# Seven-product block matmuls in fp32r pairs: the last four products of 31 output pairs take the high and low part of h side by side in one 512-column matmul

## The chip, the cores and the metric

One core of a Trainium2 chip runs the program. The metric is the device time of one execution in microseconds; three timed runs of the kernel before are given. Inputs lie in device memory as fp32, transposed and cut into tiles on the host beforehand.

## The reference, cut to what matters

```python
h = rmsnorm(x, norm_g[l])                       # x: 512 tokens x 2048
(a_q, a_ckv, i_q, i_k, i_w, a_gate, b_q, b_k, b_v, b_gate,
 c_q, c_gate, mix_gate) = split_cols(h @ w_in[l], IN_SIZES)
...
oa = dsa_attention(qa, ka, va, iq, ik, iw, bias_a, topk) * jax.nn.silu(a_gate)
ob = sliding_window_attention(qb, kb, vb, sinks_b[l], bias_b) * jax.nn.silu(b_gate)
oc = memory_attention(qc, kc, vc) * jax.nn.silu(c_gate)
g_a, g_b, g_c = jnp.split(jax.nn.sigmoid(mix_gate + gate_bias[l]), N_BRANCH, axis=-1)
merged = g_a * (oa @ w_up_a[l]) + g_b * (ob @ w_up_b[l]) + g_c * (oc @ w_up_c[l])
x = x + merged @ w_o[l]
```

Most of the arithmetic is `h @ w_in`: 2048 by 11856 weights on 512 tokens. The change is in that product.

## The kernel before

**Precision.** Every fp32 operand of a large product is split into a high part, rounded to fp32r, and a low part, the rest. A product of two such operands is three matmuls: high x high, high x low, low x high (`mm3`, lines 293 to 296: L294 is wh with the high part of h, L295 wh with its low part, L296 wl with the high part). Weights are split as they stream in (`split`): ACT rounds a 128x512 piece to `wh` (L276) and DVE subtracts to get `wl` (L278), four pieces ahead of TensorE (`LA = 4`), six buffers each.

**Seven products.** Outputs come in pairs of two 128-row tiles (transposed: rows are output columns of w_in, columns are tokens). `pair` splits the pair and the 2048-long contraction into 2x2 blocks and forms them from seven block products instead of eight (`PRODS`): each product is 8 k-tiles of 128, three matmuls of 256 columns each, so 168 matmuls a pair. The weight sums that the scheme needs (S1 to S4, tiles `wS`, `wA`, `wraw`) are made on the way in, by POOL (L212) and by accumulating DMAs that POOL issues (L218). Four products read `hth`/`htl` (h itself and one difference), three read the `hx` tiles, six 256-column slots for each of 8 k-tiles: slots 0 to 2 high, 3 to 5 low parts of the sums T2, T3, T4.

The products take the three PSUM banks a, b, c in turn, in the first 256 columns of each. Products 0 to 2 open a bank; 3 to 5 add on top of 0 to 2; 6 opens one again. After each product `evac` (lines 792 to 810) takes what it needs: product 0 is copied to u1 and product 2 to u5 (ACT), product 1 gives u2 (DVE, L796); product 3 is copied to the first half of the first output (ACT, L801); product 4 gives u3 (DVE, L804), and POOL the second half of the second output (L805); product 5 plus u2 is the second half of the first output and product 6 plus u3 the first half of the second (both DVE, L790, in `add`). Then `fin` goes on: for a gate pair two tanh (ACT, L1232) and two DMAs; for a pair of branch A or B tanh and product (L915, L916), the casts of q (L837 to L840 for B), and the head's attention.

**Order of the work.** `STREAM` is the list of pairs: 1 + 4 pairs for keys and index queries, 4 for branch C, 6 for A and 6 for B, and 24 gate pairs (`mix`) in between and behind. Attention (`a_unit`, `b_unit`, `c_unit`), the top-k selection and smaller chores are generators, advanced one step after each half product by `pump`; a table of delays (`LG`) says how many steps a generator waits between its operations. An evacuation is put off by one half product (`pend`, `flush`): the instructions of product n's evacuation stand after the first half of product n+1 in the order of every engine. Each engine runs its instructions in program order, so a wait on ACT or DVE holds up what stands behind it.

In B's stage the attention of a head stands partly in its own pair and mostly in the gate pair that follows: scores on PE, then L1122 to L1126 on DVE (scale and bias, maximum, sink), exponentials on ACT (L1128), normalising on DVE (L1131 to L1134), transposes on PE (L960), the copy to PT on ACT (L963), and PE's PT,vb matmuls (L299). In A's stage L1023 to L1031 do the same, with the score row normalised at L1031.

Of the kernel before, what the change touches and what calls it, by code (L numbers as in the profile page):

```python
# [12 lines left out]
F32R = mybir.dt.float32r  # L13
# [98 lines left out]
def hybrid_layer(ctx: ExitStack, tc: tile.TileContext, xT, memT, memR, w_g1, w_un, w_up, params, consts, rel1, onehot, out):  # L112
# [24 lines left out]
    def psum(tag, name="p"):  # L137
        return ps.tile([128, 512], F32, tag=tag, name=nm(name), bufs=2 if tag == "qk" else 1)
# [20 lines left out]
    gk = cst.tile([128, 3], F32, name="gk")  # L159
    nsink = cst.tile([128, HB], F32, name="nsink")  # L160

    hth = hp.tile([128, KT, T], F32R, name="hth")
    htl = hp.tile([128, KT, T], F32R, name="htl")
    hxt, hxf = {}, {}

    def hx_new(k, dt):
# [126 lines left out]
    def mm3(o, ah, al, bh, bl, first, last, n1=None):  # L293
        pe.matmul(o, ah, bh, start=first, stop=False, skip_group_check=True)  # L294
        pe.matmul(o, ah, bl, start=False, stop=False, skip_group_check=True)  # L295
        pe.matmul(o, al, bh, start=False, stop=last, skip_group_check=True)  # L296
# [39 lines left out]
    def tl(tag, shape=(128, 512), dt=F32):  # L336
        return ws["pool"].tile(list(shape), dt, tag=tag, name=nm(tag), bufs=ws["bufs"][tag])
# [393 lines left out]
    def hpart(name, k):  # L731
# [6 lines left out]
        i = int(name[1]) - 2  # L738
        return hxt[k][:, i, :], hxt[k][:, 3 + i, :]

    prod = [0]
    pend = []

# [33 lines left out]
            onto(x1[:, lo], p, dve)  # L777
            put(1, lo)

    def pair(z0, z1, fin, onto=None):  # L780

        ev = {}
        o = {}

        def e(name):
            ev[name] = stp("ev").tile([128, 256], F32, tag="ev", bufs=4, name=nm(name))
            return ev[name]

        def add(t, p, u):
            dve.tensor_tensor(out=t, in0=p, in1=ev[u], op=ALU.add)  # L790

        def evac(n, p):
            if n == 0:
                act.copy(e("u1"), p)
            elif n == 1:
                dve.tensor_tensor(out=e("u2"), in0=ev["u1"], in1=p, op=ALU.subtract)  # L796
            elif n == 2:
                act.copy(e("u5"), p)
            elif n == 3:
                o[0] = z0()  # L800
                act.copy(o[0][:, :256], p)  # L801
            elif n == 4:
                o[1] = z1()
                dve.tensor_tensor(out=e("u3"), in0=p, in1=ev["u1"], op=ALU.subtract)  # L804
                pool_e.tensor_tensor(out=o[1][:, 256:], in0=ev["u3"], in1=ev["u5"], op=ALU.subtract)  # L805
            elif n == 5:
                add(o[0][:, 256:], p, "u2")
            else:
                add(o[1][:, :256], p, "u3")
                fin(o[0], o[1])  # L810

        bank = {}
        for n, (_, hn, first) in enumerate(PRODS):
            b = "abc"[prod[0] % 3]
            prod[0] += 1
            if first:
                bank[b] = psum(b)[:, :256]
            p = bank[b]
            for half in range(2):
                wh, wl = next_hb()  # L820
                for kk in range(4):
                    k = 4 * half + kk
                    s = slice(kk * 128, kk * 128 + 128)
                    bh, bl = hpart(hn, k)
                    mm3(p, wh[:, s], wl[:, s], bh, bl, first and k == 0, k == 7)
                flush()
                pump()
            if onto:
                pend.append(lambda n=n, p=p: evac_add(n, p, ev, *onto))
            else:  # L830
                pend.append(lambda n=n, p=p: evac(n, p))

    def stack(z, tag):

# [341 lines left out]
    for n, item in enumerate(STREAM):  # L1176
        kind = item[0]
        if n == last:
            flush()
            pump.drain()  # L1180
            ws["stack"].close()
            ws.clear()
            switch("fp", {"t2": 4, "og": 1, "m": 2, "f": 1, "oxh": 1, "oxl": 1})
            oxh, oxl = tl("oxh", (128, 6, T), F32R), tl("oxl", (128, 6, T), F32R)
            ox = [(oxh[:, k, :], oxl[:, k, :]) for k in range(6)]
            pump.back(o_load("c", ox[:4]))
        if item[0] not in ("mix", "iq") and item[-1] in ("bkv", 0):
            flush()
        if item == ("iq", 0):
            flush()  # L1190
            pump.drain()
            ck_s.close()
            switch("iq", {"t2": 4, "stk": 6, "rl": 2, "mr": 2})
            pump.back(g_mem())
            pump.back(g_index())
            pump.back(g_ik())
            pump.back(g_rel())
        elif item == ("c", 0):
            switch("c", {**BASE, "q": 2})
        elif item == ("a", 0):  # L1200
            pump.drain()
            ws["stack"].close()
            cs_s.close()
            ws.clear()
            pump.gap = LG["gapa"]
            switch("a", {**BASE, "q": 2, "T": 2, "kv": 2})
        elif item == ("b", 0):
            pump.drain()
            ws["stack"].close()
            tk_s.close()  # L1210
            ws.clear()
            switch("b", {**BASE, "q": 4, "T": 2, "kb1": 1, "kb2": 1, "vb": 1})
            pump.gap = LG["gapb"]
            pump.back(b_start())
        if kind == "bkv":
            pair(t2, t2, kv_b)
        elif kind == "iq":
            def fin(z0, z1, item=item):
                st = [stack(z, "stk") for z in (z0, z1)]

                def ready():
                    yield from lag("iq")
                    for x in range(2):
                        j = 2 * item[1] + x
                        iq[2 * j], iq[2 * j + 1] = st[x]
                pump.back(ready())
            pair(t2, t2, fin)
        elif kind == "mix":
            def fin(z0, z1, item=item):
                _, j, d = item  # L1230
                for x, z in enumerate((z0, z1)):
                    act.activation(z, z, AF.Tanh, bias=hb[:, 16 * j + d + x:16 * j + d + x + 1], scale=0.5)  # L1232
                    sync.dma_start(th_d[3 * (d + x) + j], z)
            pair(t2, t2, fin)
        else:
            def fin(zg, zq, item=item):
                kind, h = item
                if kind == "b":
                    Q[item] = stack(zq, "q")
                    norm_q(item, zq, blk2, 64)  # L1240
                else:
                    Q[item] = zq
                    norm_q(item, zq, ones1, 128)
                gate_fin(zg, item)
                unit, n = {"a": (a_unit, 4), "b": (b_unit, 4), "c": (c_unit, 2)}[kind]
                pump.wait.extend(unit(h, ti) for ti in range(n))
            if kind == "a":
                a_load(item[1])
            if kind == "b":
                b_load(item[1])  # L1250
            pair(t2, t2 if kind == "b" else lambda: tl("q"), fin)


    flush()
# [214 lines left out]
```

## Time and profile before

| | |
|---|---|
| timed runs | 1594.66, 1604.49, 1609.01 us (median 1604.49) |
| profiled execution, its own time | 1599.41 us |
| its span | 1597.6 us |
| mean granted TensorE clock over the span | 0.98 of full |

The page's busy times count matmuls as pipelined, each with its modelled end, so the step from one start to the next, and not the listed duration, is what a matmul costs in a row of them. Idle time of an engine is put down to what released it last.

### The profile page before, as it was taken

Reading aid. Unit: us, or ns where it says so; the run is one execution under the profiler, and the core shown is the slowest. Engines: PE = TensorE matmul, PEld = TensorE weight load, DVE = VectorE, ACT = ScalarE, POOL = GpSimd, SP = SyncE. Lnnn points to the kernel's source line nnn. Section 1 sums busy time; section 2 is a strip of 40 time slices with the busy share of each in tenths; the row PEclk is TensorE's granted clock in tenths of the full one; section 3 lists DMA queues with packets and bytes.
Section 4 is the critical chain, followed back from the end, with each engine's and each line's share of the span. In section 5 each row is a group of like instructions: output and inputs, shape, how many; then the busy total and the mean of one; then the engine's idle time right before and its main releaser. Section 6 shows DMA issues by size and latency. Waiting matters only on the chain.

```text
span 1597.6 us, 29440 instructions
## 1 busy us (share of the span) xinstructions
PE 1505.2 (94%) x11066; PEld 1423.4 (89%) x11066; DVE 1244.5 (78%) x2020; ACT 788.5 (49%) x1673; POOL 583.2 (37%) x485
## 2 busy tenths in 40 slices
PE   8978998999999999999999999999999999989999
PEld 5867988989989999999998899988989888869999
DVE  6897687999998677878777777787857567997765
ACT  6555465545445544555545555555445332434442
POOL 0014342523334334433433333333424014775454
PEclk9989999999999999999999999999999999989999
DMA  8336677355445665565645454545446655555765
GB/s 307 123 110 185 165 200 200 92 155 153 141 125 157 200 171 166 165 175 137 189 148 159 152 133 145 147 145 146 132 145 186 231 191 188 175 145 168 206 196 151
DMA packets 98792, 263.75 MB, mean 165 GB/s; under 512 B 10356, under 2 KB 23796, under 8 KB 98650
## 3 DMA queue, kind: packets, MB, share of 16 engines
q1 hardware_dynamic: 78746, 197.77, 35.4%
q0 software_dynamic: 15264, 55.58, 19.0%
q10 hardware_dynamic: 4640, 8.52, 1.9%
q8 instruction: 87, 1.43, 0.4%
q14 instruction: 55, 0.45, 0.1%
HBM read 237.12 MB, written 29.04 MB: 167 GB/s over the span
## 4 chain that ended last, share of the span: by engine, by line
PE 62%; DVE 21%; issue 5%; DMA 5%; ACT 4%; POOL 3%; SPq 0%; ACTq 0%; DVEq 0%; POOLq 0%
PE p L294 18%; PE p L296 18%; PE p L295 18%; DVE wl L278 10%; PE p L299 3%; ACT wh L276 2%; DMA hx<-in_xT 1%; DMA wA<-in_w_un 1%; DVE Wk L855 1%; PE p L960 1%; POOL wS L212 1%; DVE m L893 1%; DVE t L790 1%; DVE Wk L894 1%; DVE htl L1271 1%
## 5 line engine op out<-in xcount | busy, mean ns | idle before, releaser
L294 PE MATMUL p<-hth,wh 128*128 128x256 f32 (+1 forms) x1792 | 530.1, 296 | 8.7 <-ACT hth L1269 5.4
L296 PE MATMUL p<-hth,wl 128*128 128x256 f32 (+1 forms) x1792 | 518.9, 290 | 2.0 <-DVE wl L278 2.0
L295 PE MATMUL p<-htl,wh 128*128 128x256 f32 (+1 forms) x1792 | 518.3, 289 | 2.3 <-DVE htl L1271 2.3
L278 DVE TENSOR_TENSOR wl<-wS,wh 128x512 fp32r<-128x512 f32 x318 | 312.2, 994 | 98.6 <-ACT wh L276 95.6
L294 PE MATMUL p<-hx,wh 128*128 128x256 f32 x1272 | 373.1, 293 | 5.6 <-ACT kb L1089 3.8
L296 PE MATMUL p<-hx,wl 128*128 128x256 f32 x1272 | 365.4, 287 | 1.7 <-DVE wl L278 1.6
L295 PE MATMUL p<-hx,wh 128*128 128x256 f32 x1272 | 364.1, 286 | 0.0
L294 PEld LDWEIGHTS p<-hth,wh 128*128 128x128 f32 x1792 | 344.4, 192 | 20.0 <-ACT hth L1269 5.6
L295 PEld LDWEIGHTS p<-htl,wh 128*128 128x128 f32 x1792 | 344.3, 192 | 8.7 <-DVE htl L1271 2.6
L296 PEld LDWEIGHTS p<-hth,wl 128*128 128x128 f32 x1792 | 344.0, 192 | 7.2 <-DVE wl L278 3.4
L278 DVE TENSOR_TENSOR wl<-wraw,wh 128x512 fp32r<-128x512 f32 (+2 forms) x346 | 271.6, 796 | 88.5 <-ACT wh L276 81.4
L212 POOL TENSOR_TENSOR wS<-wS,wA 128x512 f32<-128x512 f32 x106 | 152.7, 1461 | 438.1 <-DMA wA<-in_w_un 194.4
L294 PEld LDWEIGHTS p<-hx,wh 128*128 128x128 f32 x1272 | 248.4, 195 | 11.6 <-ACT kb L1089 4.0
L276 ACT CAST wh<-wraw 128x512 fp32r<-128x512 f32 (+2 forms) x346 | 202.1, 590 | 112.6 <-PE p L295 66.3
L296 PEld LDWEIGHTS p<-hx,wl 128*128 128x128 f32 x1272 | 248.1, 195 | 3.7 <-DVE wl L278 3.5
L295 PEld LDWEIGHTS p<-hx,wh 128*128 128x128 f32 x1272 | 248.5, 195 | 1.1
L276 ACT CAST wh<-wS 128x512 fp32r<-128x512 f32 x318 | 193.0, 617 | 83.7 <-POOL wS L212 42.2
L278 DVE TENSOR_TENSOR wl<-wA,wh 128x512 fp32r<-128x512 f32 x212 | 171.8, 811 | 58.1 <-ACT wh L276 54.9
L212 POOL TENSOR_TENSOR wS<-wraw,wS 128x512 f32<-128x512 f32 x106 | 169.4, 1672 | 9.5 <-DVE wl L278 9.5
L276 ACT CAST wh<-wA 128x512 fp32r<-128x512 f32 x212 | 124.0, 618 | 88.4 <-DMA wA<-in_w_un 46.3
L306 POOL TENSOR_TENSOR r<-rv,cc 128x4 f32<-128x4 f32 (+2 forms) x30 | 40.7, 1358 | 234.1 <-DVE rv L305 234.0
L1232 ACT ACTIVATE t<-t,hb 128x512 f32<-128x512 f32 x48 | 34.7, 724 | 102.5 <-DVE t L790 96.5
(224 smaller groups left out, 2017.3 us busy)
## 6 DMA issues: line engine op xcount, KB each, us to landing
wraw<-in_w_un SPq DMA_DIRECT2D x132, 512.0 KB, 5.5
wS<-in_w_un SPq DMA_DIRECT2D x53, 512.0 KB, 5.8
wA<-in_w_un SPq DMA_DIRECT2D x53, 512.0 KB, 3.7
wS<-in_w_un POOLq DMA_DIRECT2D x53, 512.0 KB, 7.6
wA<-in_w_un POOLq DMA_DIRECT2D x53, 512.0 KB, 5.2
th_d<-t SPq DMA_DIRECT2D x48, 256.0 KB, 4.6
t<-th_d SPq DMA_DIRECT2D x48, 256.0 KB, 2.9
wraw<-in_w_up SPq DMA_DIRECT2D x32, 384.0 KB, 3.6
```

The costliest lines, as they stand in the source:

```text
L212: pool_e.tensor_tensor(out=tiles_[key][:, s], in0=tiles_[a][:, s], in1=tiles_[b][:, s], op=op)
L276: act.copy(h[:, :w], s)
L278: e.tensor_tensor(out=l[:, :w], in0=s, in1=h[:, :w].bitcast(F32), op=ALU.subtract)
L294: pe.matmul(o, ah, bh, start=first, stop=False, skip_group_check=True)
L295: pe.matmul(o, ah, bl, start=False, stop=False, skip_group_check=True)
L296: pe.matmul(o, al, bh, start=False, stop=last, skip_group_check=True)
L299: pe.matmul(o, a, b, start=first, stop=last)
L306: pool_e.tensor_tensor(out=r[:, :n], in0=v[:, :n], in1=cc[:, C_NH:C_NH + n], op=ALU.pow)
L790: dve.tensor_tensor(out=t, in0=p, in1=ev[u], op=ALU.add)
L855: dve.scalar_tensor_tensor(s, rl[:, :w], iwt[:, ti, h:h + 1], s, op0=ALU.mult, op1=ALU.add)
L893: dve.max(out=m8, in_=s)
L1232: act.activation(z, z, AF.Tanh, bias=hb[:, 16 * j + d + x:16 * j + d + x + 1], scale=0.5)
```

## The change

The high and low parts of h become the two halves of one tile, so that one access pattern covers the same 256 columns of both. In products 3 to 6 of a pair with `wide` set, one matmul of 512 columns takes `wh` with high and low part together: the high sums go to the bank's first 256 columns as before, the low sums to its second 256. The wl matmul stays, 256 columns. What L295 gave is then in the other half, and `evac` adds it on DVE with one more add per product (`low`): products 3 to 6, four adds a pair. `wide` holds for the pairs of A and B and for the gate pairs behind the last pair of C: 6 + 6 + 19 = 31 of 45 pairs; the output projection's pairs are unchanged.

```diff
-    hth = hp.tile([128, KT, T], F32R, name="hth")
-    htl = hp.tile([128, KT, T], F32R, name="htl")
+    hhl = hp.tile([128, 2, KT, T], F32R, name="hhl")
+    hth, htl = hhl[:, 0], hhl[:, 1]
...
+    def hboth(name, k):
+
+        if name in ("B11", "T1", "B21", "B22"):
+            c = 0 if name in ("B11", "B21") else 256
+            return hhl[:, :, k if name in ("B11", "T1") else 8 + k, c:c + 256]
+        return hxt[k].rearrange("p (a i) c -> p a i c", a=2)[:, :, int(name[1]) - 2, :]
+
...
-        def evac(n, p):
+        def evac(n, p, pl):
+            def low(t):
+                if pl is not None:
+                    dve.tensor_tensor(out=t, in0=pl, in1=t, op=ALU.add)
+
...
             elif n == 3:
                 o[0] = z0()
                 act.copy(o[0][:, :256], p)
+                low(o[0][:, :256])
             elif n == 4:
                 o[1] = z1()
                 dve.tensor_tensor(out=e("u3"), in0=p, in1=ev["u1"], op=ALU.subtract)
+                low(ev["u3"])
                 pool_e.tensor_tensor(out=o[1][:, 256:], in0=ev["u3"], in1=ev["u5"], op=ALU.subtract)
             elif n == 5:
                 add(o[0][:, 256:], p, "u2")
+                low(o[0][:, 256:])
             else:
                 add(o[1][:, :256], p, "u3")
+                low(o[1][:, :256])
                 fin(o[0], o[1])
...
-                bank[b] = psum(b)[:, :256]
-            p = bank[b]
+                bank[b] = psum(b)
+            p, pl = bank[b][:, :256], bank[b][:, 256:]
+            w2 = wide and n > 2
...
-                    mm3(p, wh[:, s], wl[:, s], bh, bl, first and k == 0, k == 7)
+                    if not w2:
+                        mm3(p, wh[:, s], wl[:, s], bh, bl, first and k == 0, k == 7)
+                        continue
+                    pe.matmul(bank[b].rearrange("p (a c) -> p a c", a=2), wh[:, s], hboth(hn, k), start=first and k == 0, stop=False, skip_group_check=True)
+                    pe.matmul(p, wl[:, s], bh, start=False, stop=k == 7, skip_group_check=True)
...
-            pair(t2, t2, fin)
+            pair(t2, t2, fin, wide=n > STREAM.index(("c", HC - 1)))
...
-            pair(t2, t2 if kind == "b" else lambda: tl("q"), fin)
+            pair(t2, t2 if kind == "b" else lambda: tl("q"), fin, wide=kind != "c")
```

On PE, product 4 of a pair in A's stage stands like this before (two of its k-tiles; `hx` is the k-tile's sums, `p` the bank):

```order
L294 MATMUL p_10130<-hx_917,wh_10173 128x256
L295 MATMUL p_10130<-hx_917,wh_10173 128x256
L296 MATMUL p_10130<-hx_917,wl_10174 128x256
L294 MATMUL p_10130<-hx_962,wh_10173 128x256
L295 MATMUL p_10130<-hx_962,wh_10173 128x256
L296 MATMUL p_10130<-hx_962,wl_10174 128x256
```

and so after, the two k-tiles and the next:

```order
L845 MATMUL p_9737<-hx_916,wh_9780 128x512
L846 MATMUL p_9737<-hx_916,wl_9781 128x256
L845 MATMUL p_9737<-hx_961,wh_9780 128x512
L846 MATMUL p_9737<-hx_961,wl_9781 128x256
L845 MATMUL p_9737<-hx_982,wh_9780 128x512
L846 MATMUL p_9737<-hx_982,wl_9781 128x256
```

Three instructions of 256 columns became two, of 512 and 256; PE has 992 rows fewer in all, and 124 are added on DVE.

On DVE, at the border between a gate pair and the B pair behind it, these stand before (`u` is u3, the first `t` the gate pair's first output, the second its second output):

```order
L278 TENSOR_TENSOR wl_10916<-wA_2095_10707,wh_10915 128x512
L804 TENSOR_TENSOR u_2136_10935<-p_10721,u_2099_10738 128x256
L278 TENSOR_TENSOR wl_10939<-wA_2095_10707,wh_10938 128x512
L278 TENSOR_TENSOR wl_10959<-wS_2131_10897,wh_10958 128x512
L790 TENSOR_TENSOR t_2124_10879<-p_10766,u_2108_10784 128x256
L278 TENSOR_TENSOR wl_10985<-wS_2131_10897,wh_10984 128x512
L278 TENSOR_TENSOR wl_11011<-wS_2082_10640,wh_11010 128x512
L790 TENSOR_TENSOR t_2135_10934<-p_10957,u_2136_10935 128x256
L1122 SCALAR_TENSOR_TENSOR L_11038<-p_10979,r_10763,T_10405 128x256 x2
```

and these after (line numbers of the changed kernel: 803 is the new add, 817, 798 and 1143 are 804, 790 and 1122 of before):

```order
L278 TENSOR_TENSOR wl_10452<-wA_2095_10258,wh_10451 128x512
L817 TENSOR_TENSOR u_2136_10467<-p_10272,u_2099_10289 128x256
L803 TENSOR_TENSOR u_2136_10467<-p_10272,u_2136_10467 128x256
L278 TENSOR_TENSOR wl_10472<-wA_2095_10258,wh_10471 128x512
L278 TENSOR_TENSOR wl_10488<-wS_2131_10437,wh_10487 128x512
L798 TENSOR_TENSOR t_2124_10418<-p_10317,u_2108_10335 128x256
L803 TENSOR_TENSOR t_2124_10418<-p_10317,t_2124_10418 128x256
L278 TENSOR_TENSOR wl_10511<-wS_2131_10437,wh_10510 128x512
L278 TENSOR_TENSOR wl_10533<-wS_2082_10197,wh_10532 128x512
L798 TENSOR_TENSOR t_2135_10466<-p_10486,u_2136_10467 128x256
L803 TENSOR_TENSOR t_2135_10466<-p_10486,t_2135_10466 128x256
L1143 SCALAR_TENSOR_TENSOR L_10561<-p_10505,r_10314,T_9984 128x256 x2
```

Each add follows the operation that makes its input; the rest keeps its order. The pair's first add, of product 3, stands between a wl and the line-1122 operations some ten rows earlier:

```order
L278 TENSOR_TENSOR wl_10407<-wraw_10227,wh_10406 128x512
L803 TENSOR_TENSOR t_2124_10418<-p_10222,t_2124_10418 128x256
L1143 SCALAR_TENSOR_TENSOR L_10421<-p_10385,r_10314,T_9984 128x256 x2
L1145 TENSOR_REDUCE st_10422<-L_10421 128x2
L1146 TENSOR_TENSOR st_10422<-st_10422,nsink 128x2
```

There the wl and the line-1122 pair were neighbours before.

## Rows read from the trace of the kernel before

**Rows 1.** The page's engine table: busy us (share) xinstructions.

```profile
PE 1505.2 (94%) x11066; PEld 1423.4 (89%) x11066; DVE 1244.5 (78%) x2020; ACT 788.5 (49%) x1673; POOL 583.2 (37%) x485
```

**Rows 2.** Windows: from:to, length, then the columns named.

```profile
core 0: us, PE busy (x) PEld busy (x) DVE busy (x) ACT busy (x) POOL busy (x), PEclk, DMA share, GB/s
...
538.20:844.30 306.10, 299.59 (x2439) 292.62 (x2437) 235.59 (x366) 156.91 (x361) 112.49 (x97) 1.00 0.57 166
844.30:1179.10 334.80, 316.01 (x2582) 304.09 (x2581) 260.58 (x485) 175.69 (x407) 121.25 (x98) 0.98 0.51 146
```

**Rows 3.** PE's waits, 844 to 1180 us: total us, times, longest.

```profile
PE p L299 <- ACT PT L963: 12.4, 6, 2.1
PE p L296 <- DVE wl L278: 1.3, 6, 0.2
```

**Rows 4.** PE's waits, 538 to 844 us.

```profile
PE p L960 <- DVE L L1031: 5.6, 5, 1.1
```

**Rows 5.** DVE's timeline, 1049 to 1057 us: start, us, operation, [idle before].

```profile
1049.01 0.42 DVE L804 TENSOR_TENSOR u<-p,u 128x256 f32<-128x256 f32 x1
1049.34 0.68 DVE L278 TENSOR_TENSOR wl<-wA,wh 128x512 fp32r<-128x512 f32 x1
...
1051.09 0.41 DVE L790 TENSOR_TENSOR t<-p,u 128x256 f32<-128x256 f32 x1
1051.42 3.57 DVE L278 TENSOR_TENSOR wl<-wS,wh 128x512 fp32r<-128x512 f32 x2
1054.92 0.41 DVE L790 TENSOR_TENSOR t<-p,u 128x256 f32<-128x256 f32 x1
1055.26 0.86 DVE L1122 SCALAR_TENSOR_TENSOR L<-p,r,T 128x256 f32<-128x256 f32 x2
1056.15 0.69 DVE L1124 TENSOR_REDUCE st<-L 128x2 f32<-128x512 f32 x1
```

**Rows 6.** ACT's timeline in the same stretch.

```profile
1051.59 0.72 ACT L1232 ACTIVATE t<-t,hb 128x512 f32<-128x512 f32 x1 [1.88 <-DVE t L790]
1055.43 0.72 ACT L1232 ACTIVATE t<-t,hb 128x512 f32<-128x512 f32 x1 [3.11 <-DVE t L790]
1056.06 0.57 ACT L963 COPY PT<-p 128x512 f32<-128x512 f32 x1
```

**Rows 7.** PE's timeline, quiet A pair: first and last of 19 matmul starts.

```profile
552.72 0.28 PE L295 MATMUL p<-htl,wh 128*128 128x256 f32 x1
...
554.88 0.28 PE L295 MATMUL p<-htl,wh 128*128 128x256 f32 x1
```

**Rows 8.** PE's timeline, 512 columns, up projection: first and last of 18 starts.

```profile
1250.11 0.39 PE L295 MATMUL p<-oxl,wh 128*128 128x512 f32 x1
...
1253.96 0.39 PE L294 MATMUL p<-oxh,wh 128*128 128x512 f32 x1
```

**Rows 9.** POOL's timeline in the stretch of rows 5.

```profile
1051.86 1.98 POOL L212 TENSOR_TENSOR wS<-wraw,wS 128x512 f32<-128x512 f32 x1
1054.48 1.65 POOL L212 TENSOR_TENSOR wS<-wraw,wS 128x512 f32<-128x512 f32 x1 [0.64 <-DVE wl L278]
```

**Rows 10.** DVE's timeline, start of the gate pair at 1024.8 us.

```profile
1025.03 0.42 DVE L790 TENSOR_TENSOR t<-p,u 128x256 f32<-128x256 f32 x1 [0.22 <-PE p L296]
...
1031.02 0.16 DVE L305 TENSOR_SCALAR rv<-p 128x8 f32<-128x8 f32 x1
```

**Rows 11.** POOL's timeline, the same pair.

```profile
1031.26 2.05 POOL L306 TENSOR_TENSOR r<-rv,cc 128x8 f32<-128x8 f32 x1 [7.32 <-DVE rv L305]
```

**Rows 12.** DVE's timeline, later in the same pair.

```profile
1042.72 0.68 DVE L278 TENSOR_TENSOR wl<-wraw,wh 128x512 fp32r<-128x512 f32 x1
1043.33 0.86 DVE L1122 SCALAR_TENSOR_TENSOR L<-p,r,T 128x256 f32<-128x256 f32 x2
```

**Rows 13.** DVE's timeline in an A round, 725 us.

```profile
724.22 0.41 DVE L790 TENSOR_TENSOR t<-p,u 128x256 f32<-128x256 f32 x1
724.55 4.71 DVE L278 TENSOR_TENSOR wl<-wS,wh 128x512 fp32r<-128x512 f32 x2
729.19 0.41 DVE L790 TENSOR_TENSOR t<-p,u 128x256 f32<-128x256 f32 x1
```

**Rows 14.** Windows, columns as in rows 2: behind a wait; two B pairs.

```profile
901.90:905.50 3.60, 3.48 (x20) 3.15 (x21) 1.89 (x8) 3.15 (x11) 0.00 (x0) 0.54 0.80 221
...
894.90:922.20 27.30, 25.26 (x201) 24.12 (x202) 23.27 (x41) 14.32 (x33) 11.35 (x10) 0.94 0.52 142
946.80:972.70 25.90, 23.83 (x202) 22.83 (x202) 22.41 (x40) 14.20 (x33) 10.90 (x10) 1.00 0.51 143
```

More of the change, by code (lines that the diff above doesn't have):

```diff
@@ L778, in evac_add, with pair @@
             put(1, lo)
-    def pair(z0, z1, fin, onto=None):
+    def pair(z0, z1, fin, onto=None, wide=False):
         ev = {}
@@ L830, in pair @@
             else:
-                pend.append(lambda n=n, p=p: evac(n, p))
+                pend.append(lambda n=n, p=p, pl=pl: evac(n, p, pl if wide else None))
     def stack(z, tag):
```

## The prediction

> **What bounds the kernel now.** I read the page's engine table first, then the windows by stage, then TensorE's timeline in a quiet stretch, its waits, and last the timelines of the engines it waits for. The engine table says PE is busy 94% of the span, DVE 78%, ACT 49% [rows 1]. The windows say the same of the two long stages in which 26 of the 31 changed pairs lie: between 538 and 844 us (branch A's stage, 13 pairs) PE is busy 299.6 of 306.1 us and DVE 235.6; between 844 and 1179 us (branch B's, 13 pairs) 316.0 and 260.6 of 334.8 us [rows 2]. So TensorE sets the time, and a shorter matmul stream is worth something; but DVE is the engine that gets more work, so what counts is where PE already waits for it.
>
> PE's waits in these stages are few and at fixed places. In B's stage PE waits six times before the PT,vb matmuls for ACT's copy of PT, 12.4 us together, and six times for DVE's wl, 1.3 us together [rows 3]. In A's it waits five times, 5.6 us together, for DVE's row of line 1031 [rows 4]. The reader is to see that each is the end of a chain through DVE, ACT and POOL. I follow one B round (a gate pair from 1024.8 us, then a B pair from 1049.5 us). On DVE, from 1048.40 us on, there is no gap: wl, the u3 of line 804, two wl, the t of line 790, two wl, again a t [rows 5]. ACT waits 1.88 us for the first t and 3.11 us for the second, then runs the two tanh and only then the PT copy at 1056.06 [rows 6], for which PE waits.
>
> **The change part by part.**
>
> *Removed: 992 matmuls* (8 k-tiles x 4 products x 31 pairs), each with its weight load; 992 others become 512 columns wide. The 256-column matmuls of a quiet stretch start 2.16 us apart over 18 steps, 0.120 us each [rows 7]; the 512-column ones 3.85 us over 17 steps, 0.2265 us [rows 8]. Per k-tile that is 3 x 0.120 = 0.360 before and 0.2265 + 0.120 = 0.3465 after: 13.5 ns, 0.43 us per pair, 13.4 us in all. That is the most the change can give. No row shows a 512-column operand read in two halves far apart; from the contiguous rows I take 0.2265, with 0.240 (two of 256, no gain) as the other end.
>
> The Trainium skill ("TensorE: Matmul & The Clock Gate", Back-to-back issue gap) speaks against the change here: it puts the gap at N/2.4 plus 2.5 ns, 109 ns for 256 columns and 216 for 512, so that merging two would save 2.5 ns, an estimate of 2.5 us for the 992. The rows give 120 and 226.5 ns, so the trace does not agree, and I keep 13.5 ns.
>
> *Added: 124 DVE adds of 128x256* (four per pair) of the bank's other half, PSUM plus SBUF. Their nearest kin is the t of line 790, 0.41 us [rows 5]. What follows on DVE without need of such a result starts earlier than its end: u3 at 1049.01, the next wl at 1049.34, 0.33 us. What needs it starts just after its end: the second of the line-1122 operations ends at 1056.12, the reduce of its result starts at 1056.15 [rows 5]. So an add behind the operation that makes its input (u3, and both t) costs 0.46 + 0.33 - 0.33 = 0.46 us of DVE's time; the first of the four, whose input ACT copied long before, 0.33 us. That is 31 x (3 x 0.46 + 0.33) = 53 us more DVE time. By totals it fits: 13 pairs x 1.71 = 22 us on 260.6 of 334.8 us. In pairs whose DVE work has room it is hidden behind PE's matmuls and costs nothing; I take that for 15 or so of the gate and A pairs, and for the three pairs after 1179 us. If that cover were gone, each would cost up to 1.7 us.
>
> *Where it is not hidden: the B round, six times.* Three adds fall in the gapless stretch [rows 5]. The one behind u3 holds POOL's t<-u,u, its two DMA issues and its sums on wS behind them. The one behind the first t I cost at nothing: the two wl behind it take 3.57 us, against 0.68 for one uncrowded, while POOL's sum of 1.98 us runs [rows 5, 9], so DVE stands there for POOL anyway. The one behind the second t delays ACT's second tanh. Together 2 x 0.46 = 0.92 us more wait before PT,vb (0.46 if the first is hidden too, 1.38 if none is).
>
> The Trainium skill ("SBUF — State Buffer", Who interferes with whom) has a reason: a DVE operation with two SBUF inputs and a GpSimd operation that reads SBUF exclude each other, one with a single SBUF input does not take part. By it the new adds are never stretched by POOL, as the t at 1051.09 (0.41 us beside a POOL issue) bears out; but whoever starts first gets the port. Should the delayed wl always lose its place once more, the third add counts too and the sum is 11 x 0.46 = 5 us higher.
>
> The six waits for wl end another chain, through the gate pair: the last t of the pair before (1025.03), ACT's casts of it, DVE's q, G and so on with no slack up to rv at 1031.02 [rows 10], POOL's r of 2.05 us behind it [rows 11], later a wl at 1042.72 and, right behind it, line 1122 [rows 12]. The pair before now has an add behind that t (0.46), and this pair's first add goes in between the wl of 1042.72 and line 1122 (0.33): 0.79 us (0 to 0.8). So a B round grows by 0.92 + 0.79 = 1.71 us, six rounds by 10.3 us (2.8 to 13).
>
> *The A round, five times.* The same stretch (u3, wl, wl, t, wl, wl, t) stands in front of line 1031's row. The two wl behind the first t take 4.71 us there [rows 13], held up by POOL's sums too, so here as well the adds of u3 and of the last t count and the middle one does not; the first of the four comes ahead of another wl that POOL holds, and I cost it at nothing: 0.92 us each, 4.6 us (2.3 to 8).
>
> *Gain that is lost.* Where PE waits at the end of a chain, arriving earlier only lengthens the wait. So the gate pairs' 0.43 us in those eleven rounds buy nothing: 4.8 us of the 13.4. What is left is 8.6 us.
>
> **Sum:** 10.3 + 4.6 - 8.6 = +6.3 us. The profiled execution took 1599.4 us (span 1597.6 and 1.8 around it), the three timed runs 1594.7, 1604.5 and 1609.0; the mean of the four is 1601.9. I put the sum on that rather than on the low profiled one: 1608 us.
>
> **The rivals.**
>
> *The gain stays (1590 us).* If DVE's idle time takes all 124 adds, PE loses nothing: 1601.9 - 13.4 = 1588.5, with a little lost 1590. For it: DVE idles 74 us in B's stage [rows 2]. Against it: that idle time lies where DVE waits for ACT, not in the stretch of rows 5.
>
> *The longer waits cost the clock too (1620 us), the slower side.* Behind the wait before PT,vb of the B pair from 894.9 us the granted clock is 0.54 for 3.6 us, almost all at 1.2 GHz; that pair takes 27.3 us, and the one from 946.8 us, with the same kind of wait and the clock at 1.00, 25.9 [rows 14]: 1.4 us. The first is one of three such among the six. If the other three and the five of the A rounds, 2 us long instead of 1.1, do it as well, 8 x 1.4 = 11 us come on top: 1608 + 11 = 1619, 1620 with the DVE terms at their upper half. It decides from about five more such stretches on. Against it: the A waits leave the clock at 1.00 now [rows 2].
>
> *The wide matmul gives less (1616 us).* If the split operand streams at 0.240 us, nothing offsets the 14.9 us of waits: 1601.9 + 14.9 = 1617, and a part of the gain kept brings 1616. By the Trainium skill's gap (above) it would be 1617 - 2.5, some 1614, an estimate.
>
> **How the numbers follow.** The forecast gets 0.57, with a range of its own from 1601 to 1615; the kept gain 0.15, the clock 0.20, the weak matmul 0.08. A run of this kernel can be told from no change at about 1%, 16 us. Faster than that (under 1588) needs the whole gain and a low run: 0.04. Slower (over 1620.5): 0.13 out of the clock's 0.20, 0.04 from the upper tails of the others: 0.17. The rest, 0.79, is within 1%. The range for 8 in 10 reaches into both sides, 1591 to 1625.
>
> **What would show it.** Right: 256- and 512-column steps of 0.120 and 0.2265 us in the changed products; a quiet pair of 20.16 us (168 x 0.120) down to 19.7; six waits before PT,vb grown from 2.1 to 3 us or more, the five at line 1031's row (now 1052) from 1.1 to 2; DVE's busy time up by some 50 us. Wrong: waits unchanged and pairs shorter throughout (the gain stays); more stretches at the 1.2 GHz level (the clock); steps of 0.24 us (the weak matmul).

## The result, and the profile after

The changed kernel took 1620.92 us (median of four runs, 1619.42 to 1626.6), the kernel before 1603.8 beside it (1594.66 to 1609.01). The ratio is 1.0126, 95% interval [1.0092, 1.016]: slower, by about 1%. That is 17 us by the medians where the prediction put 6.3. The time lies in the range for 8 in 10 (1591 to 1625), near its upper end, and outside the forecast's own range (1601 to 1615). The profiled execution took 1622.28 us, its span 1620.4, 22.8 more than before. By stage the span went, in us (each from its first matmul to that of the next, the output's to its last):

```
pairs          before    after    difference
ahead of 0     137.37   137.71     +0.3
0 to 13        354.16   354.05     -0.1
14 to 28 (A)   352.75   358.14     +5.4
29 to 41 (B)   334.85   350.02    +15.2
42 to 44        68.01    67.59     -0.4
up projection  174.11   174.09      0.0
output         172.75   175.18     +2.4
```

The page's engine table, which answers to [rows 1]:

```profile
PE 1506.1 (93%) x10074; PEld 1373.8 (85%) x10074; DVE 1273.2 (79%) x2144; ACT 785.6 (48%) x1673; POOL 583.9 (36%) x485
```

PE has 992 rows less and no less busy time (matmuls overlap, so that figure does not show a step); DVE has 124 more and 28.7 us more, where some 50 was named as a sign of being right. The adds themselves take 52.4 us; but DVE's wl operations, which POOL's sums hold up, took 19.0 us less in all.

**The matmul's step.** PE's timeline in the last gate pair, which waits for nothing, answers to [rows 7, 8]:

```profile
1256.91 0.40 PE L845 MATMUL p<-hhl,wh 128*128 128x512 f32 x1
1257.15 0.28 PE L846 MATMUL p<-hhl,wl 128*128 128x256 f32 x1
1257.26 0.40 PE L845 MATMUL p<-hhl,wh 128*128 128x512 f32 x1
...
1260.79 0.40 PE L845 MATMUL p<-hx,wh 128*128 128x512 f32 x1
```

From 1256.91 to 1260.79 us there are eleven k-tiles: 0.3527 us each. Over all of them the median step is 0.235 us behind a wide matmul and 0.117 behind the wl one, 0.352 against 3 x 0.120. The gain is 8 ns, not 13.5; a pair without waits went from 20.16 to 19.95 us, 0.21 and not 0.43.

**PE's waits.** B's stage first (850 to 1200 us), then A's (537 to 850), beside [rows 3, 4]:

```profile
PE p L299 <- ACT PT L984: 15.1, 6, 2.5
PE p L845 <- ACT wh L276: 6.3, 6, 1.3
...
PE p L294 <- DVE u L803: 2.7, 6, 0.5
```

```profile
PE p L981 <- DVE L L1052: 7.1, 8, 1.1
PE p L299 <- ACT PT L984: 5.6, 6, 1.0
...
PE p L294 <- DVE u L803: 1.0, 1, 1.0
```

The waits before PT,vb grew from 2.1 to 2.5 us at most, where 3 or more had been forecast. In A the longest wait for the score row (line 1052 now) stayed at 1.1 us, where 2 had been forecast, though there are eight of them for five. Instead, new or longer waits stand beside these: in B for wh and for the u that the new add writes, in A for PT (5.6 us against 0.7).

**The chain that was forecast.** DVE's timeline of a B round, beside [rows 5], and ACT's, beside [rows 6]:

```profile
1061.95 0.69 DVE L278 TENSOR_TENSOR wl<-wA,wh 128x512 fp32r<-128x512 f32 x1
1062.55 0.42 DVE L817 TENSOR_TENSOR u<-p,u 128x256 f32<-128x256 f32 x1
1063.00 0.42 DVE L803 TENSOR_TENSOR u<-p,u 128x256 f32<-128x256 f32 x1
...
1065.54 0.42 DVE L803 TENSOR_TENSOR t<-p,t 128x256 f32<-128x256 f32 x1
1065.88 3.12 DVE L278 TENSOR_TENSOR wl<-wS,wh 128x512 fp32r<-128x512 f32 x2
...
1069.37 0.42 DVE L803 TENSOR_TENSOR t<-p,t 128x256 f32<-128x256 f32 x1
```

```profile
1069.89 0.72 ACT L1253 ACTIVATE t<-t,hb 128x512 f32<-128x512 f32 x1 [3.17 <-DVE t L803]
1070.52 0.56 ACT L984 COPY PT<-p 128x512 f32<-128x512 f32 x1
```

From the wl ahead of u3 to the PT copy it took 1056.06 - 1048.40 = 7.66 us before and takes 1070.52 - 1061.95 = 8.57 now: 0.91 more, where 0.92 was forecast. The two wl behind the first t fell from 3.57 to 3.12 us, so the middle add is hidden here, as forecast. This part of the sum is right to the hundredth. It is too small a part.

**The whole round.** A B round is a gate pair and a B pair. Its beat can be read off `rv`, which DVE writes once a round. DVE's rv rows of before, then of after:

```profile
L305 DVE TENSOR_SCALAR rv<-p x6: 156/158/159, 876.7 to 1133.1; 128x8 f32<-128x8 f32 x6
```

```profile
L305 DVE TENSOR_SCALAR rv<-p x6: 158/162/164, 883.6 to 1152.7; 128x8 f32<-128x8 f32 x6
```

Six starts, five rounds between them: (1133.1 - 876.7) / 5 = 51.28 us before, (1152.7 - 883.6) / 5 = 53.82 after. The round grew by 2.54 us, six of them make the 15.2 of B's stage, and the forecast said 1.71.

The missing part lies in the B pair. Its end, from its u3 to rv, reads so on DVE in the last round of before, in a round of after, and in one of the changed kernel without product 5's add (experiment 3):

```profile
1123.46 0.41 DVE L804 TENSOR_TENSOR u<-p,u 128x256 f32<-128x256 f32 x1
...
1133.06 0.16 DVE L305 TENSOR_SCALAR rv<-p 128x8 f32<-128x8 f32 x1
```

```profile
1033.58 0.41 DVE L817 TENSOR_TENSOR u<-p,u 128x256 f32<-128x256 f32 x1
...
1044.55 0.16 DVE L305 TENSOR_SCALAR rv<-p 128x8 f32<-128x8 f32 x1
```

```profile
1037.77 0.41 DVE L817 TENSOR_TENSOR u<-p,u 128x256 f32<-128x256 f32 x1
...
1048.30 0.16 DVE L305 TENSOR_SCALAR rv<-p 128x8 f32<-128x8 f32 x1
```

It takes 9.60 us before and 10.97 after: 1.37 more, three times 0.46. So all three adds count here, that behind u3, product 5's and product 6's; without product 5's it is 10.53. In the gate pair product 5's add was hidden because DVE stood for POOL's sums; here no such sum runs beside the two wl behind the first t, and they take 1.28 us before and after.

Who holds the round is told by DVE's own waits in those five rounds, before and after:

```profile
DVE wl L278 <- ACT wh L276: 40.0, 29, 2.5
DVE q L839 <- ACT q L837: 4.0, 5, 1.0
DVE G L916 <- ACT G L915: 2.1, 5, 0.4
DVE wl L278 <- PE p L296: 2.1, 1, 2.1
DVE u L796 <- PE p L296: 1.3, 2, 0.7
DVE t L790 <- PE p L296: 0.4, 2, 0.2
```

```profile
DVE wl L278 <- ACT wh L276: 43.1, 27, 2.5
DVE q L860 <- ACT q L858: 3.7, 5, 0.7
DVE G L937 <- ACT G L936: 2.1, 5, 0.4
DVE u L808 <- PE p L296: 0.2, 1, 0.2
```

The reader is to see who stands on the right: before, DVE waits 46 us for ACT and 3.8 for PE, after it 49 and 0.2. ACT in turn waits for DVE's `st`, in the same five rounds before:

```profile
ACT L L1128 <- DVE st L1125: 44.2, 20, 5.0
ACT t L1232 <- DVE t L790: 24.9, 10, 3.1
ACT wh L276 <- PE p L295: 16.4, 21, 1.7
```

DVE and ACT pass the work to and fro, and PE follows with some 2 us to spare in a round. (ACT does wait for PE too, to free wh, the third line, and 12.0 us for the inputs of its copies; that this does not hold the round is shown only by the clock below and by experiment 4.) In such a loop DVE's idle time is not room for more. The windows of these five rounds (sum rows, before and after) fit this: DVE's busy time grew by 13.0 us, the length by 12.7.

```profile
sum 256.40, PE 243.82 PEld 234.29 DVE 202.35 ACT 136.00 POOL 93.22; mean PE 48.76 PEld 46.86 DVE 40.47 ACT 27.20 POOL 18.64
```

```profile
sum 269.10, PE 247.16 PEld 220.83 DVE 215.39 ACT 135.57 POOL 92.51; mean PE 49.43 PEld 44.17 DVE 43.08 ACT 27.11 POOL 18.50
```

**The clock.** Half-clock stretches became more frequent in B's stage: 23.9 us of them against 13.7. But look at the lengths of three rounds after, one with such a stretch, one without, one with two:

```profile
937.20:990.90 53.70, 49.50 (x341) 44.50 (x340) 43.12 (x87) 27.16 (x64) 18.50 (x15) 0.97 0.50 138
990.90:1044.50 53.60, 49.38 (x351) 44.25 (x350) 42.99 (x86) 27.54 (x65) 18.51 (x15) 1.00 0.51 138
1044.50:1099.00 54.50, 49.41 (x325) 43.78 (x324) 43.17 (x86) 26.72 (x63) 18.49 (x15) 0.94 0.50 136
```

One stretch (clock 0.97) costs nothing, two (0.94) cost 0.9 us. PE had the time to spare. The kernel of experiment 2 that is wide from the first B pair on bears this out: its five rounds take 53.64 to 53.70 us, three without a stretch and two with one. In the kernel before, with PE closer behind, a stretch was not free: two rounds with one took 51.6 us, three without 50.7 to 51.3, and the difference lies in the B pair's end, 10.5 us instead of 9.6 to 9.9.

### The profile page after: what moved, and what is told of

Read it like the earlier page. It is cut to its first block, busy times and chain, and to the rows that moved or that the text cites. A ratio compares the mean times of both kernels' runs of the same rounds, so it can differ in the third digit from the quotient of the medians.

```text
span 1620.4 us, 27575 instructions
## 1 busy us (share of the span) xinstructions
PE 1506.1 (93%) x10074; PEld 1373.8 (85%) x10074; DVE 1273.2 (79%) x2144; ACT 785.6 (48%) x1673; POOL 583.9 (36%) x485
## 5 line engine op out<-in xcount | busy, mean ns | idle before, releaser
L294 PE MATMUL p<-hhl,wh 128*128 128x256 f32 (+1 forms) x1296 | 388.5, 300 | 9.8 <-ACT hhl L1290 5.4
L295 PE MATMUL p<-hhl,wh 128*128 128x256 f32 (+1 forms) x1296 | 380.1, 293 | 2.3 <-DVE hhl L1292 2.3
L296 PE MATMUL p<-hhl,wl 128*128 128x256 f32 (+1 forms) x1296 | 380.2, 293 | 1.0 <-DVE wl L278 1.0
L294 PEld LDWEIGHTS p<-hhl,wh 128*128 128x128 f32 x1296 | 251.2, 194 | 21.5 <-ACT hhl L1290 5.6
L295 PEld LDWEIGHTS p<-hhl,wh 128*128 128x128 f32 x1296 | 250.9, 194 | 8.6 <-DVE hhl L1292 2.6
L296 PEld LDWEIGHTS p<-hhl,wl 128*128 128x128 f32 x1296 | 250.8, 193 | 5.6 <-DVE wl L278 1.7
L294 PE MATMUL p<-hx,wh 128*128 128x256 f32 x776 | 227.3, 293 | 3.5 <-DVE t L770 3.5
L296 PE MATMUL p<-hx,wl 128*128 128x256 f32 x776 | 223.8, 288 | 0.3 <-DVE wl L278 0.2
L295 PE MATMUL p<-hx,wh 128*128 128x256 f32 x776 | 223.4, 288 | 0.0
L845 PE MATMUL p<-hx,wh 128*128 128x512 f32 x496 | 184.3, 409 | 10.9 <-ACT wh L276 6.3
L845 PE MATMUL p<-hhl,wh 128*128 128x512 f32 x496 | 182.8, 407 | 4.6 <-ACT u L810 3.2
L294 PEld LDWEIGHTS p<-hx,wh 128*128 128x128 f32 x776 | 152.3, 196 | 6.5 <-ACT wh L276 3.8
L296 PEld LDWEIGHTS p<-hx,wl 128*128 128x128 f32 x776 | 152.5, 196 | 0.7 <-DVE wl L278 0.7
L295 PEld LDWEIGHTS p<-hx,wh 128*128 128x128 f32 x776 | 152.6, 197 | 0.3
```

The source lines that it names most:

```text
L845: pe.matmul(bank[b].rearrange("p (a c) -> p a c", a=2), wh[:, s], hboth(hn, k), start=first and k == 0, stop=False, skip_group_check=True)
```

## The experiments

Ratios are to the kernel before, measured on the same chip, with 95% intervals; "round" is the rv beat as above. Rounds and stages come from one profiled execution of each kernel, and stages that no edit here alters differ from one to the next: the part ahead of pair 0 took 133.3 to 139.0 us, pairs 0 to 13 took 352.9 to 356.6.

**1. Which half of the change costs?** First the wide matmuls without the four adds (the low sums are then missing from the output), then the adds with the three 256-column matmuls kept, the second of them writing the other half.

```diff
-                low(o[0][:, :256])
...
-                low(ev["u3"])
...
-                low(o[0][:, 256:])
...
-                low(o[1][:, :256])
```

> The wide matmuls without the four adds: the low sums of products 3 to 6 in the 31 pairs stay in the bank's other half and are left out of the result. Theory (the loss is in the adds, which stand in chains that TensorE waits for): the waits before PT,vb stay at about 12.4 us in six, and what is left is the matmuls' gain, 7 to 13 us, ratio to before 0.992 to 0.996. Rival (the loss is in the wide matmul itself, its split operand, or the one tile that replaces two): no gain, ratio 1.000 to 1.012.

```diff
-                    pe.matmul(bank[b].rearrange("p (a c) -> p a c", a=2), wh[:, s], hboth(hn, k), start=first and k == 0, stop=False, skip_group_check=True)
+                    pe.matmul(p, wh[:, s], bh, start=first and k == 0, stop=False, skip_group_check=True)
+                    pe.matmul(pl, wh[:, s], bl, start=False, stop=False, skip_group_check=True)
```

> Three matmuls of 256 columns as before, but the high-by-low one writes the bank's other half, and the four adds fetch it. Theory: all of the loss and none of the gain: 17 us more as measured plus the 7 to 13 us that the matmuls had given back, ratio 1.015 to 1.019. Rival (loss in the matmul): ratio 1.000 to 1.003.

Matmuls alone: 1605.63 us, 1.0023 [1.0000, 1.0045]. Adds alone: 1621.54 us, 1.0114 [1.0069, 1.0159], as much as the whole change, less than this expectation had put. Their round is 54.46 us by the mean, but four of the five hold two half-clock stretches; the fifth takes 53.67, as in the changed kernel. So the loss is the adds', and the wide matmuls bring nothing even without them: A's stage went down by 1.9 us, but the round of B grew to 53.04 (in the slowest of the ten executions, 1611.71 us). There the chain to the PT copy was 7.65 us in two rounds and 8.74 to 8.77 in four, which no added work explains (see 3).

**2. Where?** Wide only in the 15 pairs ahead of the first B pair, then only from it on.

```diff
-            pair(t2, t2, fin, wide=n > STREAM.index(("c", HC - 1)))
+            pair(t2, t2, fin, wide=STREAM.index(("c", HC - 1)) < n < STREAM.index(("b", 0)))
```

> Wide products and adds in the 15 pairs ahead of the first B pair only. Theory (loss is where TensorE already waits, most of it in the B rounds): a third of the loss, +3 to +7 us, ratio 1.002 to 1.004. Rival (adds cost alike in every pair): half of 17 us, +8, ratio 1.005.

> Wide products and adds in the 16 pairs from the first B pair on. Theory: two thirds or more of the loss, +11 to +16 us, ratio 1.007 to 1.010, with the waits before PT,vb at 15 us in six and those at the next weights as in the changed kernel. Rival (alike in every pair): +9 us, ratio 1.0055.

1615.41 us, 1.0071 [1.0047, 1.0096], against 1620.37, 1.0104 [1.0074, 1.0133] (the second with n > the index of the first B pair; the other call, of the pairs of A and B, is restricted in the same way). Both halves cost more than forecast. A's stage took 358.88 us in the first and 353.76 in the second, B's 338.11 and 349.57: A's loss comes with A's adds, most of B's with B's. By the medians, though, the two losses add up to 30 us and not to the 17 of the whole change, and why is open.

**3. Which adds?** Each kernel leaves out one or two adds (their low sums are missing from the output); for u3:

```diff
-                low(ev["u3"])
```

> The changed kernel without product 4's add (behind u3); its low sums are left out of the result. Theory: this add stands in front of POOL's t<-u,u and of everything behind it, so a B round from wl to the PT copy falls from 8.57 us back by 0.46 to about 8.1, and the kernel gains 5 us (11 rounds) or more where a half-clock stretch goes with it: ratio to before 1.006 to 1.010. Rival (DVE has room there): no change, 1.0126.

> The changed kernel without product 5's add (behind the first t); its low sums are left out of the result. Theory: DVE stands behind POOL's sums there, so the stretch from wl to the PT copy stays at 8.5 to 8.6 us, and the kernel changes by 0 to 2 us: ratio 1.011 to 1.0126. Rival (every add on this stretch counts 0.46 us): 8.1 us and 5 us less, as for the add of product 4.

> Leaves out one of the four adds, that of product 6 (its low sums are not in the output). Theory that the adds count one by one along the chain: the B round loses 0.46 us before the second tanh and 0.46 us at the end of the pair before, the A round 0.46: 6 x 0.92 + 5 x 0.46 = 7.8 us less than the changed kernel, ratio to the kernel before 1.006 to 1.010. Rival, that one add taken away only moves the order in which DVE and POOL meet (as the runs without the add of u3 and of product 5 gave 1.013 and 1.016): ratio 1.011 to 1.017, with a long wl in some rounds.

> Leaves out the adds of u3 and of product 6 (their low sums are not in the output). One-by-one theory: both terms of the B round's chain are gone (0.92 us), and 0.46 of the next chain; A's 0.92 too: 6 x 1.38 + 5 x 0.92 = 12.9 us less than the changed kernel, ratio 1.002 to 1.006, chain from the wl ahead of u3 to the PT copy 7.65 us as in the kernel before. Rival (order of DVE and POOL): 1.008 or more, with chains that differ from round to round.

```
left out   time us   ratio [95%]              round   chain to PT, six times    B pair's end   A's stage
nothing    1620.92   1.0126 [1.0092, 1.016]   53.82   8.57                      10.97          358.1
u3         1622.59   1.0129 [1.01, 1.0157]    53.56   8.10 three, 9.22 three    10.52          356.6
5          1627.72   1.016 [1.0134, 1.0186]   53.70   8.57                      10.52          361.6
6          1613.74   1.0082 [1.0052, 1.0111]  52.74   8.10                      10.51          355.3
u3 and 6   1610.26   1.0056 [1.0038, 1.0074]  51.92   7.65                      10.06          351.6
```

(B pair's end: from its u3 to rv; without u3's or product 5's add as in three of the five rounds, in the other two, with two half-clock stretches, 11.0 to 11.1.)

The gate pair's chain gives back 0.46 us for each add that stood on it, and none for product 5's; the B pair's end gives back 0.45 for each of the three. So u3 and 6 count twice in a round, 5 once. Single rounds show it better than the mean (the shortest alike ones of the five, from one rv to the next):

```
left out   round, us        less than 53.66   adds that count
nothing    53.63 to 53.68   -                 -
u3         52.74 to 52.77   0.91              2 x 0.46
5          53.20 to 53.23   0.44              0.46
6          52.71 to 52.74   0.93              2 x 0.46
u3 and 6   51.80 to 51.81   1.86              4 x 0.46
```

From 51.80 to the undisturbed round of before, 50.72, is 1.08: product 5's add (0.46) and the first add twice (0.33 each) make 1.12. So the expectations of the last two, which count the adds one by one, held, by the times and by the rounds; and A's loss is gone as well when u3 and 6 are left out.

That u3 alone brought nothing to the time, and product 5's alone a loss, needs something else. For u3 it is the three gate pairs with a chain of 9.22. Here is DVE at the end of such a gate pair in the kernel without u3's add, then POOL beside it:

```profile
1009.09 0.42 DVE L803 TENSOR_TENSOR t<-p,t 128x256 f32<-128x256 f32 x1
1009.43 4.77 DVE L278 TENSOR_TENSOR wl<-wS,wh 128x512 fp32r<-128x512 f32 x2
```

```profile
1009.90 1.21 POOL L218 DMA_DIRECT2D wS<-in_w_un  x1
1010.46 3.18 POOL L212 TENSOR_TENSOR wS<-wraw,wS 128x512 f32<-128x512 f32 x2
```

Now the first wl gets through ahead of POOL (0.68 us), the second meets both of POOL's sums and takes 4.18. In the changed kernel the first meets one sum and the second passes between the two, 3.12 us for both. Half a microsecond earlier on DVE became 1.65 us later. The Trainium skill ("SBUF — State Buffer", Who interferes with whom) says that a DVE operation with two SBUF inputs and a GpSimd operation that reads SBUF exclude each other, the second to start being blocked. These rows agree that they exclude each other: the wl ends at 1014.20, 0.56 us behind POOL's last sum. They do not agree on who is blocked: the second wl starts at 1010.03 and POOL's first sum at 1010.46 (spans on POOL are rough), and it is DVE that is held up; in [rows 5, 9], too, the wl of 1051.42 starts ahead of the sum of 1051.86. What decides it is not shown.

For product 5's add this doesn't hold: the chain is as in the changed kernel, and three rounds are 0.44 us shorter. The other two, with two half-clock stretches each, took 54.36 and 54.51 us, and its stage of A took 3.5 us more; why, I did not find out.

**4. Is it ACT's order?** A theory was that the PT copy stands behind the two tanh on ACT, and that this order alone holds the round. The tanh were put two steps later, in the changed kernel, in the kernel before, and in that with the wide matmuls alone.

```diff
-                for x, z in enumerate((z0, z1)):
-                    act.activation(z, z, AF.Tanh, bias=hb[:, 16 * j + d + x:16 * j + d + x + 1], scale=0.5)
-                    sync.dma_start(th_d[3 * (d + x) + j], z)
+                def later():
+                    yield from lag(2)
+                    for x, z in enumerate((z0, z1)):
+                        act.activation(z, z, AF.Tanh, bias=hb[:, 16 * j + d + x:16 * j + d + x + 1], scale=0.5)
+                        sync.dma_start(th_d[3 * (d + x) + j], z)
+                pump.back(later())
```

> The changed kernel with the two tanh of a gate pair put off by two half products, so that ACT no longer waits for DVE's t in front of the PT copy. Theory (the B wait is that chain; the half clock follows the wait): the waits before PT,vb fall from 15 us to under 5, the half-clock stretches of the B stage from six to one or two, the adds no longer reach TensorE there, and the whole is 15 to 25 us below the changed kernel, ratio to before 0.995 to 1.003. Rival (PT waits for something else): unchanged, 1.0126.

> The kernel before with the same two tanh put off in the same way. Theory: the waits before PT,vb (12.4 us) and with them three half-clock stretches (4 us) go, 10 to 16 us in all, ratio 0.990 to 0.994. Rival: unchanged, 1.000.

> The wide matmuls without any of the adds (low sums left out), and the gate pair's two tanh put two steps later in the order, so that ACT's PT copy is not behind them. The kernel before with the same late tanh stood at 0.9966. Theory that the matmul gain is 6.6 us (quiet pair 0.21 us shorter, 31 pairs) and that the wide matmuls alone gave it back at the wait before PT,vb: with that wait gone it comes through, ratio 0.991 to 0.994. Rival, that the DVE and POOL loop holds the rounds whatever ACT's order: 0.995 to 1.001, with PE waiting for a wl or a t instead of for PT.

The theory fell. The changed kernel took 1627.68 us, 1.0149 [1.0126, 1.0173]; its PT waits are gone, and PE's waits in B read, as their first lines:

```profile
PE p L845 <- ACT wh L276: 7.3, 6, 1.3
PE p L845 <- DVE t L803: 5.9, 10, 1.2
```

The wait moved to the next thing that the loop delivers. The kernel before with late tanh took 1598.75, 0.9966 [0.9945, 0.9988], a little under the kernel before, a smaller gain than expected; with the wide matmuls alone, 1602.06, 1.0008 [0.9989, 1.0026]. Their rv rows, before first:

```profile
L305 DVE TENSOR_SCALAR rv<-p x6: 157/159/159, 876.1 to 1133.1; 128x8 f32<-128x8 f32 x6
```

```profile
L305 DVE TENSOR_SCALAR rv<-p x6: 154/156/157, 876.6 to 1133.3; 128x8 f32<-128x8 f32 x6
```

51.40 and 51.34 us: PE's waits for PT were removed and its matmuls shortened, and the round stayed where it was. The matmul gain buys nothing in B. (B's stage took 334.30 us with the late tanh alone, 334.85 before.)

**5. Is the step longer because the operand lies in two pieces?** The hx slots in another order, so that products 4 and 6 read one contiguous piece; 3 and 5 still two (what writes the slots is reordered with it, not shown).

```diff
-        return hxt[k].rearrange("p (a i) c -> p a i c", a=2)[:, :, int(name[1]) - 2, :]
+        i = int(name[1]) - 2
+        return hxt[k][:, 2 * i:2 * i + 2, :]
```

> The changed kernel with the hx slots in another order, so that the high and the low part that products 4 and 6 read lie side by side (512 columns in one piece); products 3 and 5 still read two pieces 32 KB apart. Theory that reading two pieces makes the wide matmul longer: products 4 and 6 step by 0.2265 us, 3 and 5 still by 0.235, a quiet pair 0.13 us shorter, ratio 1.009 to 1.011. Rival, that the order of a 512- and a 256-column matmul in turn sets it: 0.234 and 0.117 in all four products, ratio 1.011 to 1.015.

1622.17 us, 1.0134 [1.0097, 1.017]. PE's timeline at the border of products 5 (hhl, two pieces) and 6 (hx, one piece):

```profile
1264.48 0.40 PE L849 MATMUL p<-hhl,wh 128*128 128x512 f32 x1
...
1264.83 0.40 PE L849 MATMUL p<-hx,wh 128*128 128x512 f32 x1
...
1265.18 0.40 PE L849 MATMUL p<-hx,wh 128*128 128x512 f32 x1
```

0.35 us per k-tile on both sides; the medians are 0.235 and 0.117 for either. The pieces are not it. What makes the wide step 0.235 beside a narrow one, and 0.2265 in a row of its kind, is open.

## Why the prediction was right and wrong

- **The bound.** "TensorE sets the time ... what counts is where PE already waits" was right in A's stage, half right in B's. PE's table of waits shows where a loop touches PE, not how much of the loop is there. The prediction did say, against its first rival, that DVE's idle time "lies where DVE waits for ACT"; but it followed only the stretches that end at PE's waits. That idle time is the loop itself: 46 us for ACT against 3.8 for PE.
- **The B round, +10.3 us; measured +15.2.** This is the step that failed: "in pairs whose DVE work has room it is hidden". What was priced was priced right (0.92 in the gate pair, by the timeline; 0.46 and 0.33 behind the border). But the sum had u3, 6 and the first add of the gate pair and, of the B pair, 6 alone: 1.71 us. The B pair's u3, 5 and first add were put at nothing without a reason, and they count in full: 0.46 + 0.46 + 0.33 = 1.25 more, 2.96 in all. From the undisturbed round of before (50.72) to the usual one of after (53.63 to 53.68) it is 2.91 to 2.96. That the mean grew by less, 2.54, is because the other rounds of before held waits of their own of up to 0.9 us, which the longer loop covers.
- **The gain, -8.6 us kept.** Mis-sized twice. The 13.5 ns are 8 by the steps (6.6 by the quiet pair, 0.21 us over 32 k-tiles), and where DVE holds both pairs of a round, neither pair's gain is kept (51.40 and 51.34 us in experiment 4); the prediction had written off only the gate pair's. The weak matmul had a rival's place (0.08) and was half true: 8 ns, where it had none. The Trainium skill's gap ("TensorE: Matmul & The Clock Gate", Back-to-back issue gap), by which merging saves 2.5 ns (an estimate from its formula), errs to the other side of the 8: neither it nor the trace's uniform rows gave the step of a mixed row.
- **The A round, +4.6 us before the gain.** The stage grew by 5.4, but not where forecast. In the four rounds from 580.5 us on, DVE's first wait and the stage's length read so before, and then so after:

```profile
DVE wl L278 <- ACT wh L276: 40.3, 28, 2.3
...
580.50:772.20 191.70, 186.65 (x1515) 181.65 (x1512) 149.90 (x232) 97.54 (x228) 70.19 (x60) 1.00 0.57 165
```

```profile
DVE wl L278 <- ACT wh L276: 36.1, 28, 2.3
...
581.90:775.00 193.10, 184.59 (x1259) 167.77 (x1257) 153.92 (x265) 97.09 (x228) 71.88 (x60) 1.00 0.59 164
```

  Here DVE's wait shrank by 4.2 us while its work grew by 4.0: real room, unlike in B, where the same wait rose from 40.0 to 43.1. That the work grew by 4.0 only is POOL's doing: the 32 adds take 13.5 us, but the wl operations together fell from 102.9 to 94.9, so much of the adds stands where DVE had stood for POOL's sums. These rounds are only 0.35 us longer each. The rest fell on pairs 16 and 17 (+2.5 us) and 26 (+2.2), where waits for u (1.0 us) and PT (1.0) appeared; the prediction had taken pairs without waits to be safe.
- **The clock.** There were more half-clock stretches in B's stage, though only 17.0 us of them in the kernel that is wide from B on, with the same rounds; their price, 1.4 us each, did not hold: 0 for one in a round, 0.9 for two. The 1.4 was the difference of two pairs; the rounds of before differ by 0.3 to 0.9. A stretch in which PE would have waited anyway is free.
- **The output projection, +2.4 us,** was not forecast. It is not shown to be the change's: the stage's pairs are unchanged, and over all the profiles here it took from 172.75 us (before) to 178.07, with 173.49 in the kernel with the adds alone and 175.44 in that with the wide matmuls alone.
- **The range.** That the time lies in it is in part luck. The forecast's own range ended at 1615; what reached up to 1625 was the clock rival, whose 1620 the time met, and the clock is not what cost it.
- **The verdict.** "Within 1%" had 0.79 and "slower" (over 1620.5) 0.17. The median, 1620.92, lies on that border, and the ratio's interval reaches from 0.9 to 1.6%: slower than before for certain, over 1% probably.

## What to carry to other kernels

Before adding work to an engine with idle time, read that engine's own waits, and those of the engine it waits for: where the two wait for each other, the idle time can be the loop's latency, and then each added operation lengthens the round, in every pair that the loop runs through, except where DVE stood for a third engine anyway. Measure the loop by the beat of an operation that occurs once a round; if it does not move when the bound engine gets faster or slower (a shorter matmul, a half-clock stretch), that engine is not the bound there. Read single rounds beside the mean, since a disturbed round on either side hides what an operation costs. And step times taken from rows of one kind did not hold for a mix of two kinds.

## What the runs showed of the hardware that was not expected

- A 512- and a 256-column fp32r matmul in turn step by 0.235 and 0.117 us, where rows of one kind step by 0.2265 and 0.120; whether the wide operand lies in one piece or two makes no difference.
- Taking 0.42 us of work off DVE ahead of two contended wl made them 1.65 us longer together (3.12 to 4.77) in three of six gate pairs, since they met POOL's sums in another order.
- A wl that started 0.43 us ahead of POOL's sum was still the one held up, until 0.56 us behind the end of POOL's second sum.
- A stretch of 3.4 us at the lower clock level lengthened a round by nothing where PE had time to spare, and by 0.3 to 0.9 us where it had little.
